# A smaller descriptor ring, its space given to buffers, and the loads and passes of the v part dealt out anew

## The chip, the cores and the metric

The kernel runs on one core of a Trainium2 chip. The metric is the device time of one execution in microseconds, the median of several runs. Engines: PE multiplies matrices (PEld loads its weights), DVE, ACT and POOL work on tiles, SP issues DMAs; ACT and POOL issue DMAs too, in the order of their own instructions.

## The reference

One step of a decoder layer for 512 prompt tokens and 64 sample tokens, width 2048: a modulation from a conditioning vector, an RMSNorm, an input projection, a gated linear recurrence and a short convolution, an output projection, and then PEER, which is most of the work:

```
q = (xb @ w_q).reshape(PEER_BLOCK, PEER_HEADS, 2, HALF_DIM)
sc = jnp.einsum('thpk,pnk->thpn', q, sub_keys).astype(jnp.float32)
v1, i1 = lax.top_k(sc[:, :, 0], PEER_TOPK)
v2, i2 = lax.top_k(sc[:, :, 1], PEER_TOPK)
cand = (v1[..., :, None] + v2[..., None, :]).reshape(...)
cidx = (i1[..., :, None] * N_KEYS + i2[..., None, :]).reshape(...)
top, pos = lax.top_k(cand, PEER_TOPK)
eidx = jnp.take_along_axis(cidx, pos, axis=-1)
g = jax.nn.softmax(top, axis=-1).astype(xb.dtype)
act = jax.nn.gelu(jnp.einsum('td,thkd->thk', xb, expert_u[eidx])) * g
return jnp.einsum('thk,thkd->td', act, expert_v[eidx])
```

Each token picks 8 x 16 of 16384 experts (128 blocks of 128) and needs their rows of `expert_u` and `expert_v`, 2048 floats each. Everything is float32.

## The kernel before

The first 930 us compute modulation, projections, recurrence and the queries' input, with weights streamed through SBUF. Then come the queries and their choice of experts. PEER's rows are computed in two ways. For the 80 blocks picked most often, PE computes all 128 rows of the block for all prompt tokens (the dense way). For the other blocks, and for the sample tokens, single rows are gathered (128 rows of 8 KB in one indirect DMA on POOL, line L1203) and DVE takes the dot product or adds the weighted row (L1231 in the u part, L1258 in the v part); 223 such passes in each part.

A float32 matrix is multiplied as three products of rounded halves: a load brings a piece `raw` (SP), ACT rounds it to `xhi` (L904), POOL subtracts to `xlo` (L905), and PE multiplies xhi and xlo with the other side's `hi` and `lo`.

The u part (1200 to 2262 us) runs over 160 half steps n, each of 24 matmuls into `pu` (L1373). Beside it a table of weights per token and block is built: DVE writes one-hot tiles `op` and `wr` (L1559, `g_pair`), ACT scales `op` (L1567, `g_scale`), PE multiplies them into one bank `gbank` (L1573, `g_mm`), ACT copies the bank to `stg` (L1580, `g_out`), and DMAs take it to `gd` in memory. The list `gm` holds how far each of these has come; `LAG` is how many half steps the products stay behind the plan, `PAIRS` how many pairs may be under way. When the gathered passes come to a new set of tokens, ACT copies its row to `hT` (L1218), which waits for DVE's last pass over the old set.

The v part (from 2262 us) runs over 80 steps m of four quarter steps; a quarter step is 12 matmuls into one of four banks `pv` (L1393). Where a sum is complete, DVE adds the bank to `acc` (L1415, `v_sum`), and only then may PE use the bank again. Four blocks form a group `sg`. Its activations `actr` (from `actd`) are multiplied by its weights `gsb` (from `gd`) in `weigh` (L1336, DVE), rounded to `ahi` (L1343, ACT, `halve(sg, 0)`) and subtracted to `alo` (L1347, DVE, `halve(sg, 1)`). Each group's jobs are put at quarter steps around `h_`, the place of `halve(sg, 0)`, 16 quarter steps apart: `load_weights` in four quarters and `load_acts` in two halves, issued on ACT, and `weigh`.

Row buffers: `RB` of them in both parts, `RV` in the v part; `gather_to(n)` issues gathers up to RB - 1 (u) or RV - 2 (v) ahead of the pass and then the passes themselves. How many passes stand in a quarter step follows from `room`, a time for each quarter step. `ahead(l, c)` issues the loads of raw pieces up to l and their splits up to c; the pieces rotate through buffers in `load`.

From the queries' last head on the order of every engine's instructions is that of the program text. Each load issued by SP or ACT counts on one of eight semaphores, and it waits until the load that had this semaphore before has landed.

Of the kernel before, what the change touches and what calls it, by code (L numbers as in the profile page):

```python
# [37 lines left out]
NCH = NA // TC  # L38
QT = NA // 128
SORTED = ((0, 64, 34), (64, 128, 47), (192, 128, 37), (320, 128, 30), (448, 64, 11))  # L40
RB = 4
RV = 6
ENDS = 5
LATE = 1
PIECE = 5.5
# [2 lines left out]
PIECE_G = 6.9  # L48
HEADS_COUNTED = 4
FULL_ROWS = 1.25  # L50
LAG = 3
FIRST_G = 6
PAIRS = 6
EARLY_V = 16
KEPT = 5
PARTS = 2
HB = 4
SB = 10
# [22 lines left out]
def build(ctx, tc, A, O, dbg=None):  # L81
    nc = tc.nc
# [5 lines left out]
    ws = ctx.enter_context(tc.tile_pool(name="ws", bufs=1))  # L88
# [69 lines left out]
    p1 = ExitStack()  # L158
    c1 = p1.enter_context(tc.tile_pool(name="c1", bufs=1))
    big = p1.enter_context(tc.tile_pool(name="big", bufs=1))  # L160
    adap = p1.enter_context(tc.tile_pool(name="adap", bufs=3))
    wk = p1.enter_context(tc.tile_pool(name="wk", bufs=1))
    p1p = ExitStack()
    pp = p1p.enter_context(tc.tile_pool(name="pp", bufs=2, space=PSUM))
# [715 lines left out]
    def load(n):  # L880
        if n >= len(stream):
            return
        s = stream[n]
        k = n % 3 if n < NU2 + 2 else (n - NU2 - 2) % 4
        pool, b = (ws, 2) if k < 2 else (wx, 1) if k == 2 else (pools["vx"], 1)
        raw = pool.tile([128, 8, 128], F32, name=f"raw{n}", tag="wraw", bufs=b)
        if s[0] == "U":
            nc.sync.dma_start(raw, A["ut"][bass.ds(block(s[1]), 1), :, 8 * s[2]:8 * s[2] + 8, :].rearrange("o p k c -> p (o k) c"))
        else:
            _, i, q = s  # L890
            r2 = raw.rearrange("p (a k) c -> p a (k c)", a=2)
            for a in range(2):
                nc.sync.dma_start(r2[:, a, :], v3[bass.ds(block(i + a), 1), :, q * VC:(q + 1) * VC].rearrange("o p c -> p (o c)"))
        raws[n] = raw
# [424 lines left out]
    def load_weights(sg, q):  # L1319

        if q == 0:
            gsb[sg] = ep.tile([128, NCH, SG * TC], F32, name=f"gsb{sg}", tag="gsb", bufs=1)
        c = slice(q * NCH // GP, (q + 1) * NCH // GP)
        nc.scalar.dma_start(gsb[sg][:, c, :], gd[c, :, sg * SG:(sg + 1) * SG, :].rearrange("c p i t -> p c (i t)"))

    def load_acts(sg, q):

        if q == 0:
            acts[sg] = ep.tile([128, SG, NA], F32, name=f"actr{sg}", tag="actr", bufs=1)
        i = slice(q * SG // AP_, (q + 1) * SG // AP_)  # L1330
        nc.scalar.dma_start(acts[sg][:, i, :], actd[sg][:, i, :])

    def weigh(sg):

        a = acts[sg].rearrange("p i (c t) -> p i c t", t=TC)
        V.tensor_tensor(a, a, gsb.pop(sg).rearrange("p c (i t) -> p i c t", t=TC), op=ALU.mult)  # L1336
# [258 lines left out]
    since = None  # L1595
    spare, due_g = -BEHIND, 0.0
    R1 = R2 = None
    gm = [0, 0, 0, 0]
    ep = None

    def upto(n):
# [9 lines left out]
    for n in range(NU2):  # L1611
        _, i, c = stream[n]
        if n == 0:
            sample_twice()
        if n == 1:
            sample_rows()
        ahead(n + 3, n + 2)
        spare += PIECE if R1 is None else PIECE_G
        if R1 is not None:
            put(2)  # L1620
            g_one(n)
            if not gk:
                g_start()
            elif gm[0] < min(upto(n), gm[1] + PAIRS - 1):
                g_pair(gm[0])
                gm[0] += 2
                spare -= 2.2
            while gm[2] < gm[3]:
                g_scale(gm[2])
                gm[2] += 1  # L1630
            gm[3] = gm[0]

        even, waits = R2 is not None, False
        while spare > 0 and R2 is None:
            cost = next(steps1 if R1 is None else steps2, "end")
            if cost == "end":
                if R1 is None:
                    R1 = n
                else:
                    R2 = n  # L1640
                break
            if cost is None:
                waits = True
                break
            spare -= cost
        if not even:
            if since is None and ready[0]:
                since = n
            if since is not None and n == since + 1:
                fetch_to(RB - 1)  # L1650
            if since is not None and n > since + 2:
                due_g += RATE[R1 is not None] + (0.7 if waits and spare > 4.5 else 0.0)
            g0 = gu[0]
            gather_to(due_g, ready[0])
            if gu[0] == ready[0] and sorted_[0]:
                fetch_to(gu[0] + 1, ready[0])
            due_g = min(due_g, gu[0] + 1.0)
            spare -= 2.4 * (gu[0] - g0)
            if waits:
                spare = min(spare, 3.0)  # L1660
            G0 = gu[0]
        else:
            gather_to(G0 + (NU + EARLY_V - G0) * (n - R2) // (NU2 - 1 - R2))
        if n == E0:
            assert not pair and not stg
            put(len(puts))
            p2.close()
            epx = ctx.enter_context(ExitStack())
            ep = epx.enter_context(tc.tile_pool(name="ep", bufs=1))
        u_half(n, i, c)  # L1670
        for sg, o in ((0, 1), (1, 7)):
            d = n - E0 - o
            if 0 <= d < 2:
                load_weights(sg, 2 * d)
                load_weights(sg, 2 * d + 1)
            if 2 <= d < 4:
                load_acts(sg, d - 2)
            if d == 5 - sg:
                weigh(sg)
            if d == 6 - sg:  # L1680
                halve(sg, 0)
            if d == 7 - sg:
                halve(sg, 1)
# [8 lines left out]

    last = M - VQ - ENDS
    KQ = KD // VQ
    jobs = {}
    hi_at = -4
    for sg in range(2, L // SG):
        use = uses_of[sg * SG]
        free = KQ * (uses_of[(sg - 3) * SG][-1] + 1) if sg >= 3 else 0
        h_ = min(KQ * use[0] - 7, max(free, hi_at + 16))  # L1700
        assert h_ >= free and h_ >= hi_at + 13, (sg, h_, free, hi_at)
        for q in range(GP):
            jobs.setdefault(max(hi_at - 1 + 2 * q, 0), []).append(lambda sg=sg, q=q: load_weights(sg, q))
        for q in range(AP_):
            jobs.setdefault(max(hi_at + 6 + 2 * q, 0), []).append(lambda sg=sg, q=q: load_acts(sg, q))
        jobs.setdefault(h_ - 4, []).append(lambda sg=sg: weigh(sg))
        jobs.setdefault(h_, []).append(lambda sg=sg: halve(sg, 0))
        jobs.setdefault(h_ + 2, []).append(lambda sg=sg: halve(sg, 1))
        hi_at = h_
    room = {}  # L1710
    for m in range(last):
        for kq in range(KD // VQ):
            room[m, kq] = PIECE / 2 - 0.75 * steps[m][4] - 0.38
    tot, run_ = sum(room.values()), 0.0
    fb = finish_b()
    fplan = {(last + 1, 2), (last + 2, 3), (last + 3, 1), (last + 3, 3), (last + 4, 1), (last + 4, 3)}
# [5 lines left out]
    for m in range(M):  # L1722
        gi, q, bl, first, final = steps[m]
        n = NU2 + 2 * m
        ahead(n + 3, n + 3)
        ahead(n + 7, n + 3)
        if m == last:
            gather_to(NT)
        if m == last + 1:
# [179 lines left out]
```

## Time and profile before

| | |
|---|---|
| median of 3 runs | 3271.31 us (3267.70 to 3271.77) |
| the profiled execution's own time | 3275.15 us |
| its span | 3273.3 us |
| busy PE, PEld, DVE, ACT, POOL | 3088.6, 2616.8, 2173.3, 1056.9, 1718.4 us |
| mean granted clock of PE | 0.976 |
| DMA | 882.84 MB, mean 270 GB/s over the span |
| gathers of u and v rows on POOL | 223 and 223, mean 1021 and 1168 ns |

Busy times are unions of the instructions' times; matmuls overlap each other, so PE's busy time hides its pace, and the time from one matmul to the next is the better measure. "A <- B" in a list of waits says that A stood idle until B ended: total us, times, longest. In a row of a timeline the numbers are start and duration in us, and the bracket is the idle time before it with what ended it. A row of busy time by stretch gives the stretch, its length, each engine's busy time with its count of instructions, then the granted clock, the busy share of the DMA engines and GB/s.

### The profile page before, as it was taken

To read this page: it belongs to the slowest core of one execution; us is meant where nothing else is said; L and a number is where in the kernel's file an instruction comes from. 1 tells how busy PE (TensorE), PEld (TensorE's weight loads), DVE (VectorE), ACT (ScalarE), POOL (GpSimd) and SP (SyncE) were. 2 spreads that over 40 slices of the span, in tenths; PEclk is the share of its full clock that TensorE was granted. 3 is DMA by queue.
4 is the path that set the end of the run, shared out by engine and by line. 5 is a ranking of instruction groups with operands and counts; after the bars stand their busy time and mean duration, and the time that the engine had idled before them with its cause. 6 is when DMAs were issued, how large, how long until landed. Compare 5 with 4: busy or idle time off the path is not lost.

```text
span 3273.3 us, 46692 instructions
## 1 busy us (share of the span) xinstructions
PE 3088.6 (94%) x17239; PEld 2616.8 (80%) x17239; DVE 2173.3 (66%) x3265; ACT 1056.9 (32%) x1645; POOL 1718.4 (52%) x1000
## 2 busy tenths in 40 slices
PE   5999999999989999999999998998999999989897
PEld 2788898889979998887788787886888777777686
DVE  3465521142246898897998979856777787978755
ACT  3244311132232222222665555542222121122122
POOL 2233233344343335666556655656777676777742
PEclk9999999999989999999999999998999999999998
DMA  9744466634342228989779898989999988998964
GB/s 375 266 144 136 163 221 203 214 99 146 131 140 67 72 90 277 308 310 381 312 297 405 340 369 315 395 285 385 389 372 387 391 327 315 344 365 305 369 218 163
DMA packets 297067, 882.84 MB, mean 270 GB/s; under 512 B 37590, under 2 KB 79446, under 8 KB 245366
## 3 DMA queue, kind: packets, MB, share of 16 engines
q1 hardware_dynamic: 160608, 380.39, 33.3%
q0 software_dynamic: 66336, 413.41, 32.1%
q10 hardware_dynamic: 69888, 86.00, 7.5%
q8 instruction: 136, 2.23, 0.3%
q14 instruction: 99, 0.81, 0.1%
HBM read 879.89 MB, written 66.81 MB: 289 GB/s over the span
## 4 chain that ended last, share of the span: by engine, by line
PE 67%; DMA 15%; DVE 7%; issue 4%; POOL 4%; ACT 2%; ACTq 0%; SPq 0%; POOLq 0%; DVEq 0%
PE pu L1373 19%; PE pv L1393 14%; PE pp_o L139 6%; DMA v<-v,rows 4%; DMA gsb<-gd 4%; PE pp_c L139 3%; PE pp_s L139 3%; PE qa L139 3%; PE pp_b L139 3%; PE qb L139 3%; PE gbank L1573 2%; PE pp_x L139 2%; PE pp_y L139 2%; PE ada L189 2%; POOL xlo L905 2%
## 5 line engine op out<-in xcount | busy, mean ns | idle before, releaser
L905 POOL TENSOR_TENSOR xlo<-raw,xhi 128x1024 fp32r<-128x1024 f32 x320 | 785.6, 2467 | 453.8 <-ACT xhi L904 440.5
L904 ACT ACTIVATE xhi<-raw 128x1024 fp32r<-128x1024 f32 x320 | 338.2, 1060 | 868.6 <-PE pv L1393 353.6
L1258 DVE SCALAR_TENSOR_TENSOR accB<-v,dots,accB 128x2048 f32<-128x2048 f32 x211 | 496.3, 2352 | 159.4 <-DMA v<-v,rows 154.0
L1231 DVE SCALAR_TENSOR_TENSOR u<-u,hT 128x2048 f32<-128x2048 f32 x223 | 505.0, 2282 | 145.1 <-DMA u<-u,rows 130.2
L1393 PE MATMUL pv<-ahi,xhi 128*128 128x512 f32 x1280 | 514.8, 402 | 43.7 <-DVE acc L1415 33.7
L1393 PE MATMUL pv<-ahi,xlo 128*128 128x512 f32 x1280 | 510.8, 399 | 10.7 <-POOL xlo L905 10.5
L1373 PE MATMUL pu<-hhi,xhi 128*128 128x512 f32 x1280 | 516.9, 404 | 1.6 <-ACT xhi L904 1.6
L1373 PE MATMUL pu<-hhi,xlo 128*128 128x512 f32 x1280 | 504.7, 394 | 6.5 <-POOL xlo L905 6.5
L1393 PE MATMUL pv<-alo,xhi 128*128 128x512 f32 x1280 | 507.7, 397 | 0.0
L1373 PE MATMUL pu<-hlo,xhi 128*128 128x512 f32 x1280 | 506.0, 395 | 0.0
L1203 POOL DMA_INDIRECT u<-u,rows x223 | 227.6, 1021 | 207.1 <-DVE u L1231 155.2
L1393 PEld LDWEIGHTS pv<-ahi,xhi 128*128 128x128 f32 x1280 | 244.3, 191 | 107.8 <-DVE acc L1415 24.8
L1393 PEld LDWEIGHTS pv<-ahi,xlo 128*128 128x128 f32 x1280 | 244.1, 191 | 72.1 <-POOL xlo L905 15.1
L1203 POOL DMA_INDIRECT v<-v,rows x223 | 260.4, 1168 | 77.9 <-issue 36.3
L1373 PEld LDWEIGHTS pu<-hhi,xlo 128*128 128x128 f32 x1280 | 242.7, 190 | 61.7 <-POOL xlo L905 7.4
L1393 PEld LDWEIGHTS pv<-alo,xhi 128*128 128x128 f32 x1280 | 244.6, 191 | 54.7
L1373 PEld LDWEIGHTS pu<-hhi,xhi 128*128 128x128 f32 x1280 | 243.3, 190 | 52.5 <-ACT xhi L904 2.1
L1373 PEld LDWEIGHTS pu<-hlo,xhi 128*128 128x128 f32 x1280 | 243.0, 190 | 47.8
L1567 ACT ACTIVATE op<-op,it 128x128 f32<-128x128 f32 x512 | 155.9, 389 | 82.5 <-DVE op L1559 82.5
L1573 PEld LDWEIGHTS gbank<-wr,op 128*128 128x128 f32 x1024 | 134.4, 193 | 42.5 <-ACT stg L1580 33.1
L1573 PE MATMUL gbank<-wr,op 128*128 128x80 f32 x1024 | 133.6, 274 | 25.7 <-ACT stg L1580 25.5
L128 POOL TENSOR_TENSOR wlo_q<-raw_q,whi_q 128x1024 fp32r<-128x1024 f32 x28 | 67.8, 2420 | 142.5 <-ACT whi_q L126 142.5
(481 smaller groups left out, 5452.2 us busy)
## 6 DMA issues: line engine op xcount, KB each, us to landing
wa<-w_ada SPq DMA_DIRECT2D x96, 1024.0 KB
raw<-ut SPq DMA_DIRECT2D x160, 512.0 KB
raw<-v SPq DMA_DIRECT2D x320, 256.0 KB
actd<-act ACTq DMA_DIRECT2D x80, 256.0 KB
gd<-stg ACTq DMA_DIRECT2D x64, 320.0 KB
gsb<-gd ACTq DMA_DIRECT2D x80, 256.0 KB
actr<-actd ACTq DMA_DIRECT2D x40, 512.0 KB
raw_o<-w_out SPq DMA_DIRECT2D x32, 512.0 KB
```

The lines of the kernel that those rows point to most:

```text
L128: lo_engine(share).tensor_sub(lo, raw, r32(hi))
L139: PE.matmul(o, st, mv[pick](k), start=first, stop=last)
L189: PE.matmul(acc[32 * g:32 * g + 32, :], cpad[:, 4 * kq + g, :], w[:, g, :], start=kq == 0, stop=kq == 3)
L904: S.activation(hi, raw, AF.Copy)
L905: G.tensor_sub(lo, raw, r32(hi))
L1203: G.indirect_dma_start(out=out, out_offset=None, in_=src, in_offset=bass.IndirectOffsetOnAxis(ap=idx, axis=0), bounds_check=NE * 128 - 1, ...
L1231: V.scalar_tensor_tensor(r, r, 1.0, st["h"], op0=ALU.mult, op1=ALU.mult, accum_out=dots[i][:, j:j + 1])
L1258: V.scalar_tensor_tensor(st["a"], r, dots[i][:, j:j + 1], st["a"], op0=ALU.mult, op1=ALU.add)
L1373: PE.matmul(pu, st[:, kk, :], movA[mv](k), start=k == 0 and a == 0, stop=k == KD - 1 and a == 2)
L1393: PE.matmul(pv, st, mv, start=first and j == 0 and a == 0, stop=last and not end and j == SG - 1 and a == 2)
L1567: S.activation(ops[:, j0 + j, :], ops[:, j0 + j, :], AF.Copy, scale=it[2][:, b * 4 + j:b * 4 + j + 1])
L1573: PE.matmul(pg[:, j * L:(j + 1) * L], ops[:, j0 + j, :], wr[:, j0 + j, :], start=True, stop=True)
```

## The change

Numbers: the descriptor ring of POOL's DMAs gets 4 KB of each SBUF partition, where 16 KB was the default. The space goes to a fifth row buffer for both parts (RB 5, RV 7), a fourth buffer for the first part's `wa` loads, one more `op`/`wr` buffer pair (PAIRS 8) and a fifth `raw` buffer for the v part, with `ahead` one piece further. In the u part the scaling of `op` comes one half step later after DVE's writing (`gm` has a fifth place) and LAG is 4. In the v part weight quarters stand at h-1, h, h+1 and h+2 (before h-1, h+1, h+3, h+5), act halves at h+5 and h+6 (before h+6, h+8), `weigh` at h-3 (before h-4), and `room` is cut in the quarter steps of `weigh` and `alo` by WEIGH = 2.8 instead of by 0.38 in all.

```
-RB = 4
-RV = 6
+RB = 5
+RV = 7
-LAG = 3
+LAG = 4
-PAIRS = 6
+PAIRS = 8
+WEIGH = 2.8
-    adap = p1.enter_context(tc.tile_pool(name="adap", bufs=3))
+    adap = p1.enter_context(tc.tile_pool(name="adap", bufs=4))
...
-        k = n % 3 if n < NU2 + 2 else (n - NU2 - 2) % 4
-        pool, b = (ws, 2) if k < 2 else (wx, 1) if k == 2 else (pools["vx"], 1)
+        k = n % 3 if n < NU2 + 2 else (n - NU2 - 2) % 5
+        pool, b = (ws, 2) if k < 2 else (wx, 1) if k == 2 else (pools["vx"], 2)
...
-    gm = [0, 0, 0, 0]
+    gm = [0, 0, 0, 0, 0]
...
-            gm[3] = gm[0]
+            gm[3], gm[4] = gm[4], gm[0]
...
-    jobs = {}
+    jobs, busy = {}, {}
...
-            jobs.setdefault(max(hi_at - 1 + 2 * q, 0), []).append(lambda sg=sg, q=q: load_weights(sg, q))
+            jobs.setdefault(max(hi_at - 1 + q, 0), []).append(lambda sg=sg, q=q: load_weights(sg, q))
         for q in range(AP_):
-            jobs.setdefault(max(hi_at + 6 + 2 * q, 0), []).append(lambda sg=sg, q=q: load_acts(sg, q))
-        jobs.setdefault(h_ - 4, []).append(lambda sg=sg: weigh(sg))
+            jobs.setdefault(max(hi_at + 5 + q, 0), []).append(lambda sg=sg, q=q: load_acts(sg, q))
+        jobs.setdefault(h_ - 3, []).append(lambda sg=sg: weigh(sg))
...
+        busy[h_ - 3] = busy[h_ + 2] = WEIGH
...
-            room[m, kq] = PIECE / 2 - 0.75 * steps[m][4] - 0.38
+            room[m, kq] = PIECE / 2 - 0.75 * steps[m][4] - busy.get(KQ * m + kq, 0.0)
...
-        ahead(n + 7, n + 3)
+        ahead(n + 8, n + 3)
...
-    nc = _bacc.Bacc("TRN2", target_bir_lowering=False, num_devices=1)
+    nc = _bacc.Bacc("TRN2", target_bir_lowering=False, num_devices=1, dynamic_dma_scratch_size=4096)
```

Two lines are added above, so the changed kernel's line numbers are one higher from L56 and two higher from L1709. The numbers at a tile's end count up as the program is written, so they tell how old a tile is.

ACT in the u part, two half steps of before: `op` is scaled (L1567) some 66 numbers behind the newest piece.

```order
L904 ACTIVATE xhi_16525<-raw_16443 128x1024
L1585 DMA gd<-stg_16073 128x640 x2
L1580 ACTIVATE stg_16429<-gbank 128x4x80
L1567 ACTIVATE op_16459<-op_16459,it_13585 128x128 x8
L1580 ACTIVATE stg_16429<-gbank 128x4x80
L904 ACTIVATE xhi_16589<-raw_16520 128x1024
L1580 ACTIVATE stg_16429<-gbank 128x4x80
L1376 ACTIVATE act_16636<-pu_16554 128x512
```

The same place of the changed kernel:

```order
L905 ACTIVATE xhi_16579<-raw_16499 128x1024
L1586 DMA gd<-stg_16129 128x640 x2
L1581 ACTIVATE stg_16482<-gbank 128x4x80
L1568 ACTIVATE op_16444<-op_16444,it_13591 128x128 x8
L1581 ACTIVATE stg_16482<-gbank 128x4x80
L1377 ACTIVATE act_16637<-pu_16549 128x512
L1378 DMA actd<-act_16637 128x512
```

The tile that is scaled is 135 numbers older than the newest piece there: one half step more lies between DVE's writing and ACT's scaling.

ACT in the v part, the loads of one group (gsb is the weights, actr the activations; each pair of xhi is one step's splits), before:

```order
L1324 DMA gsb_23051<-gd 128x4x128
L904 ACTIVATE xhi_23066<-raw_22879 128x1024
L904 ACTIVATE xhi_23070<-raw_22888 128x1024
L1343 ACTIVATE ahi_23092<-actr_22843 128x2048
L1324 DMA gsb_23051<-gd 128x4x128 x2
L904 ACTIVATE xhi_23160<-raw_22973 128x1024
L904 ACTIVATE xhi_23164<-raw_22982 128x1024
L1324 DMA gsb_23051<-gd 128x4x128
L1331 DMA actr_23228<-actd 128x1024
L904 ACTIVATE xhi_23261<-raw_23074 128x1024
L904 ACTIVATE xhi_23265<-raw_23083 128x1024
L1331 DMA actr_23228<-actd 128x1024
```

and in the changed kernel:

```order
L1325 DMA gsb_23451<-gd 128x4x128
L905 ACTIVATE xhi_23466<-raw_23193 128x1024
L905 ACTIVATE xhi_23470<-raw_23285 128x1024
L1344 ACTIVATE ahi_23497<-actr_23225 128x2048
L1325 DMA gsb_23451<-gd 128x4x128 x3
L905 ACTIVATE xhi_23561<-raw_23294 128x1024
L905 ACTIVATE xhi_23565<-raw_23378 128x1024
L1332 DMA actr_23615<-actd 128x1024 x2
L905 ACTIVATE xhi_23667<-raw_23387 128x1024
L905 ACTIVATE xhi_23671<-raw_23474 128x1024
```

The fourth weight quarter has moved ahead of the next step's splits, and the second act half ahead of those of the step after.

DVE in the v part, from the weighting of one group (L1336, in the changed kernel L1337) to its alo, before:

```order
L1336 TENSOR_TENSOR actr_24007<-actr_24007,gsb_23826 128x2048
L1258 SCALAR_TENSOR_TENSOR accB_23889<-v_9_24080,dots_14565,accB_23889 128x2048
L1258 SCALAR_TENSOR_TENSOR accB_23889<-v_10_24098,dots_14565,accB_23889 128x2048
L1258 SCALAR_TENSOR_TENSOR accB_23889<-v_11_24155,dots_14565,accB_23889 128x2048
L1258 SCALAR_TENSOR_TENSOR accB_23889<-v_12_24174,dots_14565,accB_23889 128x2048
L1415 TENSOR_TENSOR acc<-acc,pv_4_24161 128x512
L1415 TENSOR_TENSOR acc<-acc,pv_5_24179 128x512
L1258 SCALAR_TENSOR_TENSOR accB_23889<-v_13_24192,dots_14565,accB_23889 128x2048
L1347 TENSOR_TENSOR alo_24262<-actr_24007,ahi_24261 128x2048
L1415 TENSOR_TENSOR acc<-acc,pv_6_24197 128x512
```

and in the changed kernel:

```order
L1337 TENSOR_TENSOR actr_24004<-actr_24004,gsb_23841 128x2048
L1259 SCALAR_TENSOR_TENSOR accB_23888<-v_10_24082,dots_14571,accB_23888 128x2048
L1259 SCALAR_TENSOR_TENSOR accB_23888<-v_11_24100,dots_14571,accB_23888 128x2048
L1259 SCALAR_TENSOR_TENSOR accB_23888<-v_12_24131,dots_14571,accB_23888 128x2048
L1416 TENSOR_TENSOR acc<-acc,pv_4_24180 128x512
L1259 SCALAR_TENSOR_TENSOR accB_23888<-v_13_24175,dots_14571,accB_23888 128x2048
L1416 TENSOR_TENSOR acc<-acc,pv_5_24194 128x512
L1348 TENSOR_TENSOR alo_24277<-actr_24004,ahi_24276 128x2048
L1416 TENSOR_TENSOR acc<-acc,pv_6_24212 128x512
L1416 TENSOR_TENSOR acc<-acc,pv_7_24232 128x512
```

The weighting stands one row addition later, four row additions (before five) lie between it and alo, and none now lies just after alo.

## The prediction

> **What bounds the kernel now.** I read the page first, then busy time by stretch, then the waits of one stretch, then one stall in order of time. The page:
>
> ```profile
> span 3273.3 us, 46692 instructions
> PE 67%; DMA 15%; DVE 7%; issue 4%; POOL 4%; ACT 2%; ACTq 0%; SPq 0%; POOLq 0%; DVEq 0%
> ```
>
> Two thirds of the chain is PE, so what counts is where PE loses time. The pv matmuls (L1393) by stretch, and below them all engines for the second one:
>
> ```profile
> core 0: us, PE busy (x) PEld busy (x), PEclk, DMA share, GB/s
> 2320.00:2495.00 175.00, 175.00 (x760) 142.45 (x759) 1.00 1.01 381
> 2540.00:3128.00 588.00, 542.58 (x2259) 431.19 (x2258) 0.97 0.92 341
> ...
> 2540.00:3128.00 588.00, 542.58 (x2259) 431.19 (x2258) 475.27 (x271) 120.09 (x110) 408.83 (x245) 0.97 0.92 341
> ```
>
> Undisturbed, a matmul takes 175/760 = 0.2303 us, so a quarter step of 12 takes 2.76 us. The 2259 of the second row would need 520.2 us and take 588: 67.8 us are lost there. DVE's 475 us (third figure of the last row) would fit into 520, and so would POOL's 409. DMA would not: 0.92 of 588 is 541 us.
>
> ```profile
> ACT xhi L904 <- DMA raw<-v: 144.2, 31, 21.2
> POOL xlo L905 <- ACT xhi L904: 126.6, 36, 12.8
> DVE accB L1258 <- DMA v<-v,rows: 84.9, 43, 10.0
> PE pv L1393 <- DVE acc L1415: 33.7, 18, 4.9
> PE pv L1393 <- POOL xlo L905: 9.3, 6, 3.0
> PE pv L1393 <- ACT xhi L904: 2.3, 1, 2.3
> ```
>
> These are the waits of 2540 to 3128 us. PE itself waits 45.3 us, mostly for the eviction L1415 on DVE, which stands behind row additions that wait for rows. The same chain once, around 2870 us, and what SP waited for in it:
>
> ```profile
> 2850.93 0.34 ACTq L1331 DMA_DIRECT2D actr<-actd  x1
> 2870.82 1.06 ACT L904 ACTIVATE xhi<-raw 128x1024 fp32r<-128x1024 f32 x1 [18.86 <-DMA raw<-v]
> 2871.97 5.84 POOL L905 TENSOR_TENSOR xlo<-raw,xhi 128x1024 fp32r<-128x1024 f32 x2 [12.80 <-ACT xhi L904]
> 2870.93 2.29 DVE L1336 TENSOR_TENSOR actr<-actr,gsb 128x2048 f32<-128x2048 f32 x1 [2.86 <-DMA actr<-actd]
> 2885.55 2.35 DVE L1258 SCALAR_TENSOR_TENSOR accB<-v,dots,accB 128x2048 f32<-128x2048 f32 x1 [7.67 <-DMA v<-v,rows]
> 2888.64 0.47 PE L1393 MATMUL pv<-ahi,xhi 128*128 128x512 f32 x1 [1.26 <-DVE acc L1415]
> ...
> SPq L893 <- DMA gsb<-gd: 28.1, 2, 18.3
> ```
>
> SP held back a load of raw for 18.3 us, ACT waited 18.9 for it, POOL 12.8 behind ACT, the next row gathers stand behind xlo in POOL's order, and DVE ran out of rows. Over the whole v part SP's own waits are:
>
> ```profile
> SPq L893 <- POOL xlo L905: 297.1, 101, 11.8
> SPq L893 <- DMA gsb<-gd: 266.2, 29, 18.7
> SPq L893 <- DMA actr<-actd: 39.7, 12, 13.3
> ```
>
> A raw load has no data from gsb. It waits because SP's and ACT's loads count on eight shared semaphores, and each waits until the earlier load on its semaphore has landed. The pairs can be read off the built program. An act half took 20.0 us from issue (2850.93) to use (2870.93), about seven quarter steps.
>
> **The u part.** Pu matmuls (L1373), then the small gbank matmuls (L1573) of the same stretches, then waits of 1579 to 2113 us:
>
> ```profile
> 2058.00:2168.00 110.00, 94.34 (x384) 70.48 (x385) 1.00 0.90 350
> 1579.00:2113.00 534.00, 429.70 (x1728) 319.54 (x1728) 0.98 0.90 355
> ...
> 2058.00:2168.00 110.00, 24.68 (x195) 25.34 (x194) 1.00 0.90 350
> 1579.00:2113.00 534.00, 118.43 (x909) 119.00 (x907) 0.98 0.90 355
> ...
> PE gbank L1573 <- ACT stg L1580: 24.8, 14, 5.6
> ACT op L1567 <- DVE op L1559: 66.6, 34, 4.3
> ACT hT L1218 <- DVE u L1231: 12.1, 2, 6.8
> ```
>
> The first stretch has no PE gap: 384 at 0.2303 are 88.4 us, which leaves 21.6/195 = 0.111 for a small one. The second then needs 1728 x 0.2303 + 909 x 0.111 = 498.9 and takes 534: 35 us lost. PE's gaps, 24.8 us, end with stg: one bank takes all gbank results, and ACT empties it late because it stands at op, waiting for DVE.
>
> **The change, part by part.**
>
> Scaling one turn later (gm with five places, LAG, PAIRS): no instruction more or less. ACT reaches op one turn later (a half step of u, 24 x 0.2303 = 5.5 us and more), with DVE's order unchanged; the longest of its 34 waits was 4.3 us, so they should go. Not touched are the two waits at hT, 12.1 us, which come of DVE being late with u rows; a fifth row buffer can only shorten them. So the gain lies between 0 and 35 us, is at least 24.8 - 12.1 = 12.7 if all short gaps go, and I take half of the loss: 17.7 us.
>
> v part, order of the loads. In quarter steps around the split h: weight quarters now at h-1 to h+2 (before: every second one up to h+5), act halves at h+5 and h+6 (before h+6 and h+8), and, through a fifth buffer, every second raw load now has three steps until its split instead of two. From the built programs I took each raw load of the busy part whose semaphore counted a gsb or act load before, and the planned distance from that load to the split that needs the raw. Before, 18 of 64 had eight quarter steps or fewer (median 9); now 3 of 57 (median 11). Eight are 22 us, against the 20 us that a load took. So most waits of ACT for raw should end, POOL's gathers come in time, and DVE's waits shorten. What is late next is the DMA system itself: 541 us of packets. Its share was 0.92 in this stretch and 1.01 at full pace (2320 to 2495). I take the middle, 0.97: 541/0.97 = 557.7 us, a gain of 30.3. The ends are 0 (share stays) and 52 (1.01).
>
> Rows (RB 5, RV 7) and passes by room: as many gathers and additions as before, one more row in flight; no row addition is planned in the steps of weighting and of alo. This is part of the same gain, costed at nothing by itself. Weighting a step later gives the act halves a step more to land; its price is a rival below.
>
> ```profile
> L1203 POOL DMA_INDIRECT v<-v,rows x223 | 260.4, 1168 | 77.9 <-issue 36.3 <-DVE accB L1258 28.7 <-DMA v<-v,rows 3.5
> q0 software_dynamic: 66336, 413.41, 32.1%
> PE ada L189 <- DMA wa<-w_ada: 34.9, 14, 18.2
> 100.00:120.00 20.00, 16.73 (x123) 10.47 (x121) 5.46 (x13) 3.86 (x7) 4.65 (x4) 1.00 1.04 385
> 140.00:160.00 20.00, 20.00 (x151) 18.31 (x150) 13.76 (x17) 7.74 (x11) 7.67 (x3) 1.00 0.41 148
> ```
>
> Ring of 4 KB: the program has no wait on it. The 446 gathers and a few writes moved 66336 packets, some 149 a row or 9.3 on each of 16 engines, and seven rows would hold 65 places each. Where the ring would bind no run shows, so I bound it: nothing, or, if every gather became as long as its mean grew from u to v (1021 to 1168 ns on the page), 0.15 us for each of the v part's 207 gathers, 30 us, of POOL, which has 588 - 409 us to spare. I take 0. The Trainium skill, page "DMA: Bandwidth & Descriptors", section "Terms", gives 16 bytes a descriptor: by that, as an estimate, 256 places, and the sum stays.
>
> Fourth wa buffer: PE waited 34.9 us for wa, all while the DMA share was 1.04; from 140 us on PE is full. Bytes set that stage, not buffers: 0, between -3 (a wa load ahead of a w_in load) and +5. The tail (3128 to 3273) keeps its instructions: 0 within 3.
>
> Sum on the profiled execution, 3275.15 us: 3275.2 - 17.7 - 30.3 = 3227.2. The median of the runs shown lies 3.8 lower, so the forecast is 3223.
>
> **Rivals.**
>
> 1. The loads starve. Of the 22 us from 2690 on:
>
> ```profile
> q0 software_dynamic: 1044, 7.64, 83.9%
> q10 hardware_dynamic: 897, 0.84, 11.1%
> ```
>
> Gather packets average 7.3 KB, ACT's loads 0.94 KB, and the gathers took eight times the share. A sixth row in flight could stretch a load from 20 us to over 28 (ten quarter steps); then raw is late as before, the v gain is 0 and the time 3254. For it: these rows. Against: the count of rows goes up by a fifth, 20 x 6/5 = 24 us. The Trainium skill, same page, section "Queues, rings and completion order", says an engine takes whole packets from its queues in turn; by that rule a further row gives the gathers no larger share while their queue is never empty, the load's time stays near 20 us, and the sum is as forecast.
>
> 2. Weighting too late (slower). The first weight quarter for the next group stands on ACT after the weighting and before the next pair of splits. Weighting began 17.7 us before the matmul of the next step that needs those splits (2870.93, 2888.64), planned 22.1; now 19.4 are planned. It takes 2.3 and the pair 1.06 + 2 x 2.4 = 5.9 us, so DVE may be 19.4 - 2.3 - 5.9 = 11 us late; it was 4.4. Beyond 11 us PE pays microsecond for microsecond in each of 18 groups: 3 us too much are 54, and the v gain is gone: 3254 + 54 = 3308.
>
> 3. Full DMA. At share 1.01 the v part gains 52 and the u part up to 25: 3271 - 77 = 3194.
>
> 4. It does nothing: hT holds u, the DMA share stays: about 3268.
>
> **How the numbers follow.** Forecast 0.60, rival 1 0.17, rival 3 0.07, rival 4 0.06, rival 2 0.06, and 0.04 for a ring that binds or a start that suffers (slower). Within 0.2%, 6.5 us, is what a measurement of this kernel can tell from no change: that is rival 4, 0.06. Slower 0.10, faster 0.84. The range runs from 3194 (full DMA) to 3258 (the starved case with 4 us of slack): 0.60 + 0.17 + 0.07, a little less for its edges.
>
> **What would show it.** Right: PE's wait for stg under 10 us; ACT's wait at op near 0; SP's wait for gsb under half of 266; ACT's wait for raw under 60 us; the v part's DMA share near 0.97; PE's wait for acc under 15 us. Wrong: gsb or act loads that land later than 28 us, ACT idle before xhi until DVE actr, longer gathers on POOL, or a start before 140 us that grew.

## The result, and the profile after

The changed kernel takes 3228.86 us (median of 4 runs, 3221.97 to 3229.28), the kernel before 3271.54 us on the same chip: a ratio of 0.9856, 95% interval 0.9835 to 0.9877. The quotient of these two medians alone is 0.9870, a saving of 42.7 us; the ratio on record makes it 47. Both lie in the interval. The forecast was 3223, in a range of 3194 to 3258. The profiled execution took 3228.61 us, its span is 3226.7 us. Its page, the span and the shares of the chain that ended last:

```profile
span 3226.7 us, 46647 instructions
PE 68%; DMA 15%; POOL 5%; DVE 5%; issue 5%; ACT 1%; SPq 1%; ACTq 0%; POOLq 0%; DVEq 0%
```

PE's share went from 67% to 68%, and no other engine's share rose by more than a point. To see where 46.6 us of span went, I cut at the first pu and the first pv matmul. The last two numbers of each row are the first and the last start; the first pair of rows is the kernel before, the second the changed one:

```profile
L1373 PE MATMUL pu<-hhi,xhi x1280: 387/393/774, 1200.5 to 2261.8; 128*128 128x512 f32 x183
L1393 PE MATMUL pv<-ahi,xhi x1280: 387/393/793, 2262.5 to 3247.3; 128*128 128x512 f32 x183
...
L1374 PE MATMUL pu<-hhi,xhi x1280: 387/393/774, 1193.7 to 2243.9; 128*128 128x512 f32 x183
L1394 PE MATMUL pv<-ahi,xhi x1280: 387/393/796, 2244.6 to 3200.6; 128*128 128x512 f32 x183
```

| | before | changed | gained | forecast |
|---|---|---|---|---|
| start, to the first pu | 1200.5 | 1193.7 | 6.8 | 0 |
| u part, first pu to first pv | 1062.0 | 1050.9 | 11.1 | 17.7 |
| v part, first pv to the last | 984.8 | 956.0 | 28.8 | 30.3 |
| after it | 26.0 | 26.1 | -0.1 | 0 |

**The v part.** Busy time by stretch, for the stretch at full pace and for the one after it; the first two rows count pv matmuls alone, the third all engines:

```profile
2310.00:2525.00 215.00, 215.00 (x933) 175.02 (x933) 1.00 1.00 385
2525.00:3092.00 567.00, 547.50 (x2306) 439.46 (x2305) 0.97 0.94 353
...
2525.00:3092.00 567.00, 547.50 (x2306) 439.46 (x2305) 471.72 (x274) 123.55 (x113) 400.43 (x245) 0.97 0.94 353
```

The pace is the same, 215/933 = 0.2304 us a matmul. The 2306 matmuls of the second stretch need 531 us and take 567, so 36 us are lost where 67.8 were. The waits there, and SP's waits over the whole v part:

```profile
ACT xhi L905 <- DMA raw<-v: 208.9, 39, 16.3
POOL xlo L906 <- ACT xhi L905: 117.3, 40, 9.7
DVE accB L1259 <- DMA v<-v,rows: 66.9, 52, 5.9
PE pv L1394 <- POOL xlo L906: 9.6, 6, 2.1
PE pv L1394 <- ACT xhi L905: 9.2, 6, 3.1
PE pv L1394 <- DVE acc L1416: 0.8, 2, 0.5
...
SPq L894 <- POOL xlo L906: 260.3, 88, 12.1
SPq L894 <- DMA gsb<-gd: 181.5, 23, 16.9
SPq L894 <- DMA raw<-v: 167.0, 58, 14.7
```

PE's wait for `acc` has all but gone (33.7 to 0.8 us). ACT's wait for raw has not: it is larger in sum (144.2 to 208.9), but its longest is shorter (21.2 to 16.3), and so is POOL's behind it (12.8 to 9.7). What is left reaches PE directly, as a wait for xhi or xlo.

Late rows right ahead explain only half of the wait for `acc` before. The prediction followed one of its 18 pieces, which ends at 2888.64 us behind a row addition that waited for rows. The next piece in the same trace is another kind:

```profile
2891.27 5.78 DVE L1347 TENSOR_TENSOR alo<-actr,ahi 128x2048 fp32r<-128x2048 f32 x1
2896.97 0.67 DVE L1415 TENSOR_TENSOR acc<-acc,pv 128x512 f32<-128x512 f32 x1
2897.70 0.50 PE L1393 MATMUL pv<-ahi,xhi 128*128 128x512 f32 x1 [3.25 <-DVE acc L1415]
```

The bank addition came right behind the subtraction to `alo`, which took 5.78 us where its shortest is 2.28: the pause is no longer than this difference. Nine of the 18 pieces stand behind `alo`, 17.2 of 33.7 us. What stretched `alo` is not shown, and late rows further ahead may have their part in these pieces too. In the changed kernel, where `room` keeps row additions away from `alo`, no piece is.

**The u part.** Waits from 1563 to 2094 us:

```profile
PE gbank L1574 <- ACT stg L1581: 25.3, 4, 14.1
ACT hT L1219 <- DVE u L1232: 20.7, 2, 17.7
ACT op L1568 <- DVE op L1560: 6.1, 4, 2.4
ACT hT L1219 <- DMA h2r<-h2d,tok: 4.7, 1, 4.7
```

ACT's wait at `op` fell from 66.6 to 6.1 us, as the later scaling should make it. But PE waits for `stg` as long as before, 25.3 us against 24.8, only in 4 pieces instead of 14, and ACT's wait at `hT` grew. The longest, in order of time, and behind it the busy time of PE, PEld, DVE, ACT and POOL just ahead:

```profile
1875.55 1.88 ACT L1219 ACTIVATE hT<-h2r 128x2048 f32<-128x2048 f32 x1 [17.73 <-DVE u L1232]
1879.36 0.71 ACT L1581 ACTIVATE stg<-gbank 128x320 f32<-128x320 f32 x1
1880.13 1.15 PE L1574 MATMUL gbank<-wr,op 128*128 128x80 f32 x4 [14.08 <-ACT stg L1581]
...
1836.00:1876.00 40.00, 30.05 (x156) 25.27 (x154) 39.52 (x44) 16.01 (x36) 24.10 (x18) 0.92 0.74 263
```

DVE works without a pause (39.52 of 40 us) and is behind. ACT comes to the copy of the next token set's row into `hT`, which must wait until DVE has done its last pass over the old set, and `stg` stands behind that copy on ACT.

### The profile page after: what moved, and what is told of

Same layout as the page of the kernel before. It is cut to its first block, busy times and chain, and to the rows that moved or that the text cites. A ratio compares the mean times of both kernels' runs of the same rounds, so it can differ in the third digit from the quotient of the medians.

```text
span 3226.7 us, 46647 instructions
## 1 busy us (share of the span) xinstructions
PE 3078.9 (95%) x17239; PEld 2617.8 (81%) x17239; DVE 2161.6 (67%) x3265; ACT 1052.2 (33%) x1645; POOL 1697.2 (53%) x1001
## 4 chain that ended last, share of the span: by engine, by line
PE 68%; DMA 15%; POOL 5%; DVE 5%; issue 5%; ACT 1%; SPq 1%; ACTq 0%; POOLq 0%; DVEq 0%
PE pu L1374 20%; PE pv L1394 15%; PE pp_o L140 6%; DMA gsb<-gd 5%; DMA raw<-v 5%; PE pp_c L140 3%; PE pp_s L140 3%; PE qa L140 3%; PE pp_b L140 3%; PE qb L140 3%; POOL xlo L906 2%; PE pp_x L140 2%; PE pp_y L140 2%; PE ada L190 2%; PE gbank L1574 2%
## 5 line engine op out<-in xcount | busy, mean ns | idle before, releaser
L906 POOL TENSOR_TENSOR xlo<-raw,xhi 128x1024 fp32r<-128x1024 f32 x320 | 775.1, 2432 | 497.7 <-ACT xhi L905 485.5
L1232 DVE SCALAR_TENSOR_TENSOR u<-u,hT 128x2048 f32<-128x2048 f32 x223 | 504.9, 2282 | 128.7 <-DMA u<-u,rows 116.3
L1259 DVE SCALAR_TENSOR_TENSOR accB<-v,dots,accB 128x2048 f32<-128x2048 f32 x211 | 496.3, 2352 | 110.7 <-DMA v<-v,rows 108.4
L1204 POOL DMA_INDIRECT v<-v,rows x223 | 251.5, 1128 | 59.5 <-issue 35.0
L1574 PEld LDWEIGHTS gbank<-wr,op 128*128 128x128 f32 x1024 | 135.6, 194 | 38.1 <-ACT stg L1581 27.5
L1574 PE MATMUL gbank<-wr,op 128*128 128x80 f32 x1024 | 132.2, 272 | 25.4 <-ACT stg L1581 25.3
L1416 DVE TENSOR_TENSOR acc<-acc,pv 128x512 f32<-128x512 f32 x144 | 96.7, 681 | 72.4 <-PE pv L1394 72.4
## 6 DMA issues: line engine op xcount, KB each, us to landing
gd<-stg ACTq DMA_DIRECT2D x64, 320.0 KB, 12.1
gsb<-gd ACTq DMA_DIRECT2D x80, 256.0 KB, 15.9
```

The source lines that it names most:

```text
L906: G.tensor_sub(lo, raw, r32(hi))
L1204: G.indirect_dma_start(out=out, out_offset=None, in_=src, in_offset=bass.IndirectOffsetOnAxis(ap=idx, axis=0), bounds_check=NE * 128 - 1, ...
L1232: V.scalar_tensor_tensor(r, r, 1.0, st["h"], op0=ALU.mult, op1=ALU.mult, accum_out=dots[i][:, j:j + 1])
L1259: V.scalar_tensor_tensor(st["a"], r, dots[i][:, j:j + 1], st["a"], op0=ALU.mult, op1=ALU.add)
L1416: V.tensor_add(ak, ak, pv)
L1574: PE.matmul(pg[:, j * L:(j + 1) * L], ops[:, j0 + j, :], wr[:, j0 + j, :], start=True, stop=True)
```

## Experiments

Every kernel was timed against the kernel before on its own chip; two ratios differ surely only from about 0.003 on (10 us). The kernels ran on several chips, so compare ratios, not medians: the fourth column is the difference of the ratios times 3271.54 us. By the quotient of the changed kernel's own medians (0.9870) each of its entries would be some 5 us lower. The last columns are read from the two rows shown above for before and changed.

| kernel | median us | ratio, 95% | us against the changed one | u part | v part |
|---|---|---|---|---|---|
| before | 3271.54 | 1 | +47 | 1062.0 | 984.8 |
| changed | 3228.86 | 0.9856 (0.9835 to 0.9877) | | 1050.9 | 956.0 |
| e1 old scaling | 3230.87 | 0.9855 (0.9832 to 0.9879) | 0 | 1044.2 | 963.2 |
| e2 old job times | 3251.80 | 0.9916 (0.9897 to 0.9935) | +20 | 1051.5 | 993.2 |
| e3 four raw buffers | 3239.75 | 0.9887 (0.9866 to 0.9908) | +10 | 1048.7 | 961.7 |
| e4 hT copy on DVE | 3211.64 | 0.9790 (0.9768 to 0.9812) | -22 | 1029.3 | 959.4 |
| e5 e1 and e4 | 3220.92 | 0.9832 (0.9799 to 0.9865) | -8 | 1036.3 | 950.9 |
| e6 old row places | 3248.58 | 0.9935 (0.9911 to 0.9959) | +26 | 1066.8 | 954.7 |
| e7 gsb on POOL's queue | 3216.32 | 0.9827 (0.9802 to 0.9853) | -9 | 1046.8 | 950.0 |
| e8 e4, first gsb early | 3203.91 | 0.9796 (0.9770 to 0.9822) | -20 | 1028.2 | 952.3 |
| e9 e4 and e7 | 3196.57 | 0.9760 (0.9740 to 0.9780) | -31 | 1027.1 | 950.3 |
| e10 e9 with old scaling | 3200.63 | 0.9774 (0.9754 to 0.9793) | -27 | 1032.2 | 946.8 |
| e11 before, with rows and ring | 3258.84 | 0.9950 (0.9933 to 0.9967) | +31 | 1045.9 | 988.3 |
| e12 three wa buffers | 3227.90 | 0.9863 (0.9841 to 0.9885) | +2 | 1051.3 | 960.3 |

The u part repeats well: kernels with the same u code and rows (changed, e2, e3, e7, e12) lie between 1046.8 and 1051.5. The v part of one and the same v code (changed, e1, e4, e5, e12) spreads from 950.9 to 963.2, so single v figures say little below 12 us. PE's waits at the pv matmuls, added up over a trace, part the kernels more clearly: 53.9, 58.2 and 53.4 us with the old job times (before, e2, e11), 28.7 to 39.3 in the eight with the new ones, and 26.4 to 28.0 with the weight quarters on POOL's queue besides (e7, e9, e10).

**e1: the old scaling of the u part.**

```
-LAG = 4
+LAG = 3
-PAIRS = 8
+PAIRS = 6
-    gm = [0, 0, 0, 0, 0]
+    gm = [0, 0, 0, 0]
-            gm[3], gm[4] = gm[4], gm[0]
+            gm[3] = gm[0]
```

> The changed kernel with the old scaling of the u part (gm with four places, LAG 3, PAIRS 6), all else as changed. Theory A, the later scaling took the short stalls out of the u part: the traces put 11.1 us of the gain between the first pu and the first pv matmul, so the time goes up by 9 to 13 us, to about 3240; ACT's wait at op for DVE comes back to about 60 us and PE's wait for stg is spread over a dozen gaps again, none over 7 us. Rival B, the hT copy holds the u part and the gain there came from the fifth row buffer: within 3 us of the changed kernel (3226 to 3232), with the 14 us gap still there.

No change: rival B on the time. Its u part is even 6.7 us shorter. The waits from 1200 to 2262 us:

```profile
ACT op L1568 <- DVE op L1560: 43.0, 20, 6.2
PE gbank L1574 <- ACT stg L1581: 16.7, 10, 3.5
ACT hT L1219 <- DVE u L1232: 7.6, 2, 4.3
```

The short waits at `op` are back, and the long one at `hT` has gone with the gap of 14 us, against rival B's letter. ACT and PE pay DVE's backlog either in small pieces at `op` or in one piece at `hT`.

**e4: the copy into hT on DVE.**

```
-            S.activation(st["h"], r, AF.Copy)
+            V.tensor_copy(st["h"], r)
```

> The changed kernel with the four copies of h into hT on DVE instead of ACT. In the trace of the changed kernel ACT stands 17.7 and 4.7 us at this copy, and PE's gaps at stg of 14.1 and 7.8 us end right behind it. Theory A, these gaps are made by the copy standing ahead of stg on ACT: PE's wait for stg falls from 25 to under 6 us and the time by 12 to 20 us (3209 to 3217); DVE gets 4 x 2.2 us more. Rival B, DVE is full there and everything that ACT scales is late anyway: the gaps come back as ACT's wait at op for DVE, and the time stays within 4 us (3225 to 3233).

Theory A, and a little beyond its range: 0.9790, some 22 us less, all of it in the u part (1050.9 to 1029.3). Waits from 1200 to 2262 us:

```profile
DVE u L1232 <- DMA u<-u,rows: 84.5, 54, 4.5
ACT op L1568 <- DVE op L1560: 38.1, 24, 7.6
PE gbank L1574 <- ACT stg L1581: 7.7, 5, 4.2
```

PE's wait for `stg` falls from 25.3 to 7.7 us, 17.6 of the 21.6 us by which the u part is shorter. The granted clock over it went from 0.98 to 1.00, which is where the rest may lie. Part of what ACT waited comes back at `op` (38.1 us), as rival B said, but there it seldom reaches PE: `LAG` leaves room between `op` and the product. DVE's wait for rows is 84.5 us; in the changed kernel it was:

```profile
DVE u L1232 <- DMA u<-u,rows: 116.3, 72, 13.8
```

**e5: both.** Both diffs above.

> Both edits together: the old scaling of the u part and the hT copies on DVE. The old scaling alone cost nothing (0.9855 of the time before, against 0.9856) and the copies on DVE alone gave 0.9790. Theory A, the hT copy hid the worth of the later scaling, since PE saved in short stalls what it then paid in one long one: with the copy gone from ACT the old scaling costs 10 to 18 us, so 0.982 to 0.985. Rival B, the later scaling is worth nothing here in any case, because DVE's backlog sets the pace: within 4 us of the copies on DVE alone, 0.978 to 0.980.

Undecided by the times: 0.9832 is higher than 0.9790, but the intervals overlap. The u part is 7.0 us longer than with the copy alone.

**e10: the same question on top of e9.**

> The kernel of the run before with the old scaling of the u part. Theory A, with the hT copy off ACT the later scaling is worth something: 10 to 18 us slower than the run before (0.0030 to 0.0055 more). Rival B, it is worth nothing: within 4 us (0.0012), as the profiled executions of the two kernels with the copy on DVE suggest (3209.9 and 3210.4 us of span).

0.0014 more, which no interval tells from nothing (rival B); the u part is 5.1 us longer, the same sign as in e5. So, as single traces have it: with the hT copy on ACT the later scaling costs the u part about 6 us (e1, and e6 below against the kernel before, 1066.8 to 1062.0), and with the copy gone it gives about 6.

**e6: the old row places.**

```
-RB = 5
-RV = 7
+RB = 4
+RV = 6
```

> The changed kernel with four rows in the u part and six in the v part, as before the change. Theory A, the row places are what moved the u part (the trace of the changed kernel gained 11 us there, and the scaling was shown to be worth nothing): 6 to 14 us slower, DVE's wait for u rows above 130 us instead of 116. Rival B, a row more in flight takes DMA time from the weight and act loads (rival 1 of the prediction): with a row less these land sooner (gsb below 15.9 us median) and the time falls by 3 to 10 us. Neither: within 3 us.

26 us slower, beyond theory A's range, and the trace puts 15.9 us of it in the u part. (That execution is the shortest of its six, 5 us under their median; where the rest lies is not shown.) Waits from 1200 to 2262 us, then the median landing of the weight quarters, with the old rows and with the new:

```profile
DVE u L1232 <- DMA u<-u,rows: 134.3, 83, 14.0
PE gbank L1574 <- ACT stg L1581: 33.2, 6, 15.6
ACT hT L1219 <- DVE u L1232: 28.3, 2, 19.4
...
gsb<-gd ACTq DMA_DIRECT2D x80, 256.0 KB, 14.6
...
gsb<-gd ACTq DMA_DIRECT2D x80, 256.0 KB, 15.9
```

With a row less DVE waits 18 us longer for u rows (116.3 with five places), gets further behind, and ACT stands longer at `hT`. The v part's length did not move beyond its spread, but PE's waits in it changed places: 24.7 us for `acc` against 0.8, and 9.0 for xhi and xlo against 22.6. Of the 24.7 only 3.0 lie behind `alo`; the others stand behind row additions that waited for rows. Rival B's start is right, that a row more makes the weight quarters land later: 14.6 us here, 15.3 to 16.3 in the five traces with the new rows and the same v code. Its consequence is not.

**e11: the rows and the ring on the kernel before.** RB 5, RV 7 and the ring of 4 KB.

> The kernel before with nothing but the descriptor ring of 4 KB and the row places that it pays for (five in the u part, seven in the v part). Theory A, the rows carry some 26 us by themselves, as the changed kernel lost without them: ratio 0.990 to 0.994, DVE's wait for v rows under 120 us instead of 154. Rival B, a row more only helps where raw comes in time, since gathers stand behind xlo on POOL: ratio 0.997 to 1.000, and rows and load order need each other. Rival C, a ring of 4 KB holds the gathers back: 1.000 or more, gathers above 1168 ns in the v part.

Between A and B: 0.9950, 16 us faster than before, all in the u part (1062.0 to 1045.9); the v part stays (984.8 and 988.3). The waits of the whole run, before and then with the rows, show that rows alone do not help there:

```profile
DVE accB L1258 <- DMA v<-v,rows: 154.0, 73, 10.0
...
DVE accB L1258 <- DMA v<-v,rows: 84.0, 41, 6.2
PE pv L1393 <- DVE acc L1415: 29.4, 10, 5.8
```

DVE waits 70 us less for rows, and PE still waits 29.4 us for `acc` (33.7 before). Of these, 22.0 lie behind `alo`, which took up to 7.0 us. So more rows shorten the pieces that are not behind `alo`, most of them behind late rows (16.5 us before, 7.4 here), and leave the others. Rival C falls: gathers of v rows took 1153 ns in the mean against 1168.

**e2: the old times of the v part's jobs.** Weight quarters, act halves, weighting and `room` as before; five raw buffers and seven rows stay.

```
-            jobs.setdefault(max(hi_at - 1 + q, 0), []).append(...load_weights...)
+            jobs.setdefault(max(hi_at - 1 + 2 * q, 0), []).append(...load_weights...)
-            jobs.setdefault(max(hi_at + 5 + q, 0), []).append(...load_acts...)
+            jobs.setdefault(max(hi_at + 6 + 2 * q, 0), []).append(...load_acts...)
-        jobs.setdefault(h_ - 3, []).append(lambda sg=sg: weigh(sg))
+        jobs.setdefault(h_ - 4, []).append(lambda sg=sg: weigh(sg))
-            room[m, kq] = PIECE / 2 - 0.75 * steps[m][4] - busy.get(KQ * m + kq, 0.0)
+            room[m, kq] = PIECE / 2 - 0.75 * steps[m][4] - 0.38
```

> The changed kernel with the old times of the v part's jobs (weight quarters at every second quarter step, act halves at +6 and +8, weighting at h-4, even room of 0.38 a step); the fifth raw buffer and the seven rows stay. Theory A, the order of the loads carried the v part: 20 to 29 us slower (3249 to 3258), SP's wait for gsb back over 240 us. Rival B, the fifth raw buffer carried it: 3 to 10 us slower (3232 to 3239), SP's wait for gsb between 180 and 220.

20 us slower, theory A at its lower end. Its profiled execution is the longest of its seven, 18 us over their median, so its v part of 993.2 is nearer 975 as a rule. Its waits:

```profile
SPq L894 <- DMA gsb<-gd: 320.4, 36, 22.8
PE pv L1394 <- DVE acc L1416: 46.0, 16, 6.0
```

Both are back and above those of before (266.2 and 33.7). DVE's wait for v rows is not: 64.3 us over the run, less than the changed kernel's 108.4. Of the 46.0 us, 30.5 lie behind `alo`, which took up to 7.9 us; in all traces with the new job times it is at most 5.2. The edit takes back loads, weighting and `room` together, so it does not say which of them carried the 20 us. SP's wait speaks for the loads, the waits behind `alo` for `room`.

**e3: four raw buffers.**

```
-        k = n % 3 if n < NU2 + 2 else (n - NU2 - 2) % 5
-        pool, b = (ws, 2) if k < 2 else (wx, 1) if k == 2 else (pools["vx"], 2)
+        k = n % 3 if n < NU2 + 2 else (n - NU2 - 2) % 4
+        pool, b = (ws, 2) if k < 2 else (wx, 1) if k == 2 else (pools["vx"], 1)
-        ahead(n + 8, n + 3)
+        ahead(n + 7, n + 3)
```

> The changed kernel with four raw buffers in the v part instead of five, the order of the loads as changed. Theory A, the order carried it: 3 to 10 us slower (3232 to 3239). Rival B, the buffer carried it, because raw loads are issued a step earlier: 18 to 29 us slower (3247 to 3258), ACT's wait for raw over 260 us against 230.

10 us slower by the ratios, at the edge of what two of them can tell: theory A. Rival B's sign came without its price: ACT waits 327.8 us for raw over the whole run, 230.4 in the changed kernel. The trace itself shows little: its v part is 5.7 us longer and PE's waits in it are 36.7 us, both within the spread of kernels that have the buffer.

**e7: the weight quarters on POOL's queue.**

```
-        nc.scalar.dma_start(gsb[sg][:, c, :], gd[c, :, ...
+        nc.gpsimd.dma_start(gsb[sg][:, c, :], gd[c, :, ...
```

> The changed kernel with the weight quarters gsb of the v part loaded through POOL's queue, which counts on semaphores of its own, instead of ACT's. Theory A, raw loads are late because they wait for gsb's semaphores: SP's wait for gsb goes from 181 us to near 0, ACT's wait for raw falls under half of 230, PE's waits in the v part (some 33 us from the first pv on) halve, and the time falls by 8 to 20 us, less what 80 more loads cost POOL (1 us each, 80 us, beside 167 us of slack). Rival B, the DMA system is full and raw loads are late for bandwidth: SP's wait goes, ACT's wait for raw stays over 180 us and the time within 5 us. Rival C, gsb behind the gathers in one queue lands later than 25 us and DVE's weighting waits for it: 10 to 40 us slower.

SP's waits of the v part, then ACT's for raw, and the landing of raw here and in the changed kernel:

```profile
SPq L894 <- POOL xlo L906: 393.0, 125, 11.9
SPq L894 <- DMA raw<-v: 177.1, 79, 9.2
ACT xhi L905 <- DMA raw<-v: 175.6, 42, 8.7
...
raw<-v SPq DMA_DIRECT2D x320, 256.0 KB, 14.0
...
raw<-v SPq DMA_DIRECT2D x320, 256.0 KB, 8.5
```

SP does not wait for gsb any more. The raw loads go out earlier and take longer (14.0 us instead of 8.5), so ACT's wait for raw falls by a quarter only, but its longest halves (16.3 to 8.7 us). PE's waits at pv did not halve, as theory A had it: 28.0 us against 28.7, of which 18.6 now end with `acc`. The time falls by 9 us, just inside the doubt of one comparison; e9 below repeats it. Theory A at its edge: the shared semaphores held raw loads back. That bytes are what else makes raw late, as rival B has it, fits the longer landing but was not tried, and where in PE's time the 9 us lie is not shown.

**e8: the first weight quarters earlier, with the hT copy on DVE.** The four quarters of the group whose loads all stood in the v part's first quarter step go out two half steps before the end of the u part.

> The hT copies on DVE, and besides the four weight quarters of the first group of the v part's own loop are loaded two halves before the end of the u part instead of all together in the v part's first quarter step. In the changed kernel ACT stood 10.5 us there in front of an act load that waited for gsb, and PE 5.3 us behind it; the stretch of 65.4 us holds 219 matmuls, 50.4 us at full pace. Theory A, this stall is made by the four loads at once: 5 to 12 us less than the 3211.6 of the copies on DVE alone, ratio 0.9755 to 0.9775. Rival B, the same bytes move and raw loads at the end of the u part are late instead: within 4 us.

Rival B: 0.9796 against 0.9790. In the changed kernel's trace ACT stood 10.5 us there and PE 5.3; in the trace of e4 PE lost only 2.1 us at that place, so there was little to win.

**e9: the two that helped.** The diffs of e4 and e7.

> The changed kernel with both edits that gave something: the hT copies on DVE (0.9790 of the time before) and the weight quarters gsb on POOL's queue (0.9827), against 0.9856 for the changed kernel. Theory A, they act in different parts (u and v) and add: 0.9856 - 0.0066 - 0.0029 = 0.976. Rival B, what the v part gained from gsb on POOL is lost again when the u part ends earlier, since DMA or DVE then binds: 0.978 to 0.980.

0.9760, theory A to the digit: 3196.57 us, by the ratios 31 us below the changed kernel, the fastest of this study. What PE still waits for in its v part, for the most part:

```profile
PE pv L1394 <- DVE acc L1416: 21.0, 9, 7.4
PE pv L1394 <- ACT xhi L905: 4.8, 1, 4.8
```

All of the 21.0 stand behind row additions that waited for rows, none behind `alo`, and DVE waits 149.3 us for v rows over the run, 116.3 in e4: rows bind again where raw comes sooner.

**e12: three wa buffers.** `adap` back to `bufs=3`.

> The changed kernel with three wa buffers at the start instead of four. Theory A, the buffer did what the start gained (the first pu matmul at 1193.7 us instead of 1200.5): 4 to 8 us slower, first pu after 1199 us, PE's wait for wa 34 us or more. Rival B, bytes set that stage: within 3 us, first pu below 1197.5.

Rival B: within 3 us, first pu at 1195.4 us. PE's wait for `wa` is 36.9 us, as theory A said (30.3 in the changed kernel), but the start grew by 1.7 only. All traces of the changed kernel's kin begin pu between 1193.7 and 1197.9 us, the two traces with the old code at 1200.5 and 1201.2. Part of this is there early, in the stage that reads `wa`: the last matmul into `pp_x` from `w1hs` starts at 133.9 us before, 129.7 in the changed kernel and 131.9 with three buffers. What gives the rest stays open.

## Why the prediction was right, point by point

The number was near for a reason that is half right. On the profiled execution 48.0 us were forecast, 17.7 and 30.3, and 46.6 came: 6.8 at the start, 11.1 in the u part, 28.8 in the v part. Of the six signs of being right two came, ACT's wait at `op` (6.1 us) and PE's for `acc` (0.8). Four did not: PE's wait for `stg` (25.3), SP's for gsb (181.5), ACT's for raw (208.9) and the DMA share (0.94).

- **v part, 30.3 us: right in place and size, the cause in part.** The traces give 28.8; job times and fifth raw buffer cost 20 and 10 us when undone, the second at the edge of the doubt, and without rows the v part kept its gain (954.7). The chain from late raw over late rows to PE's wait for `acc` was taken for the whole of that wait; it shows for half of it, and the other half lay right behind `alo`. Keeping row additions away from there was costed at nothing by itself, and the traces with the old job times lose 17.2 to 30.5 us at that place. The size came out with some luck, since its working was off twice, in opposite directions. The DMA share was to rise to 0.97 with the packets' time fixed; it rose to 0.94, and the packets' time itself fell from 541 to 0.94 x 567 = 533 us, for 47 matmuls more. And ACT's wait for raw did not fall under 60 us: it rose to 208.9, in shorter pieces. SP's wait for gsb fell to 181.5, not below 133.
- **u part, 17.7 us: the step that failed is "Not touched are the two waits at hT".** They were what the saved time ran into: 12.1 us became 20.7, and 4.7 for a row of h. The scaling was worth nothing (e1); moving the copy off ACT was worth 22 us (e4). The prediction held the waits of ACT apart, as if each were its own cost. Both end with DVE, and e1 and e4 show them trading places: at `op` and at `hT` ACT waits 43.0 and 7.6 us in e1, 9.7 and 20.7 in the changed kernel, 38.1 and none in e4.
- **Rows, 0 by themselves: wrong.** They carried 16 us alone (e11, all in the u part) and 26 in the company of the rest (e6, of which the trace shows 15.9 in the u part), where the prediction only said that they could shorten the waits at hT. That the total held is luck: in the u part the rows' 16 us, less the 5 to 7 that the later scaling cost, gave 11.1 in place of the scaling's 17.7, and the start's 6.8, costed at 0, made up the rest.
- **Start, 0 between -3 and +5:** it gained 6.8, of which undoing the wa buffer takes back 1.7 (e12). Of the 34.9 us that PE waited for wa, 18.2 are the wait for the very first load, and all of it ends by 97 us, ahead of the rows shown; there too the DMA share was 1.02 to 1.04, from 10 us on. **Ring, 0:** right, gathers of v rows took 1128 ns in the changed kernel, 1168 before. **Tail, 0:** right.
- **Rival 1, starving loads:** its first link holds (14.6 us in e6, 15.9 in the changed kernel) but not the time. By the count of rows a load was to take a fifth longer. By the Trainium skill, page "DMA: Bandwidth & Descriptors", section "Queues, rings and completion order", engines take packets from the queues in turn, which speaks for little change. The measured eleventh lies between.
- **Rival 2, late weighting:** its sign was ACT idle before xhi until the weighting. That was 23.2 us over the run before and 19.2 in the changed kernel, so the rival did not come. The step of weighting was not tried by itself. **Rival 3, full DMA:** the share stayed at 0.94.

## What to carry to other kernels

Where one engine is behind, take all waits of the others for it together: here a stall removed at one place came back at another instruction that needed the late engine, and the one worth moving was that which held unrelated work in its queue. Undo each part of a change by itself even when the total fits, since here a part costed at nothing stood in for a part worth nothing. Follow more than one stall of a kind, and look at what stands right before the instruction that is waited for: half of PE's wait for `acc` lay right behind a subtraction, not behind a row addition. A load that waits for nothing of its own but for a counter shared with slower loads can go to a queue with other counters; here that was worth about 0.003 of the time, in e7 and again in e9.

## What was not expected of the hardware

One late xhi cost PE some 1.7 times its pauses (6.6 us for 3.8). ACT and PE in the changed kernel, each in order of time, and then the pv matmuls of these 6.8 us as busy time by stretch (PE, PEld, granted clock, DMA share, GB/s):

```profile
2245.81 1.91 ACT L1344 ACTIVATE ahi<-actr 128x2048 fp32r<-128x2048 f32 x1 [5.64 <-DVE actr L1337]
2247.62 1.04 ACT L905 ACTIVATE xhi<-raw 128x1024 fp32r<-128x1024 f32 x1
...
2248.72 0.80 PE L1394 MATMUL pv<-ahi,xhi 128*128 128x512 f32 x1 [2.59 <-ACT xhi L905]
2251.16 0.80 PE L1394 MATMUL pv<-ahi,xlo 128*128 128x512 f32 x1 [1.22 <-POOL xlo L906]
2251.75 0.63 PE L1394 MATMUL pv<-ahi,xhi 128*128 128x512 f32 x1
...
2255.16 0.58 PE L1394 MATMUL pv<-ahi,xlo 128*128 128x512 f32 x1
...
2248.70:2255.50 6.80, 5.56 (x12) 4.01 (x13) 0.50 1.05 384
```

ACT came late to this xhi because it had stood at `ahi` until DVE's weighting was done. A late xhi stops PE twice here, at xhi and again at xlo, which POOL computes from it. After the first stop the granted clock is 0.50: from 2251.75 to 2255.16 eight matmuls start 0.426 us apart instead of 0.23. The twelve of the stretch need 12 x 0.2303 = 2.8 us at full pace and pause 1.22, so 6.80 - 2.8 - 1.2 = 2.8 us are lost to the clock, on top of 3.8 us of pauses. From 2255.50 to 2260 us the clock is 0.99 again. The Trainium skill, page "TensorE: Matmul & The Clock Gate", Part 1, has the clock fall after about 3.4 us of idling; here it fell behind a pause of 2.59. In the v stretch as a whole PE's waits are 19.6 us (9.6 + 9.2 + 0.8) of the 36 lost; as an estimate from a granted clock of 0.97 over 567 us, the other 17 or so would be the clock's.
